# Output projection of a hybrid decoder layer: embedding inputs cast later, x added to h later, the second half's squares summed as rows come, no weight sums ahead of RWKV7's inverses

## The chip, the cores and the metric

The kernel runs on one core of a Trainium2 chip. Five engines work side by side, each in the order of its own queue: TensorE (PE, matrix products, with its weight loads shown apart as PEld), VectorE (DVE), ScalarE (ACT), GpSimd (POOL) and SyncE (SP, which here only issues DMAs). ACT and POOL issue DMAs too; POOL's can add to what stands at their target ("accumulating" ones, the software queue q0). The metric is device time in microseconds, the median of several executions.

## The reference, cut to what matters

One layer, 1024 tokens of width 1024, float32:

```
z = rmsnorm(h) @ w_in                       # 30 column blocks of 128
o_a = hgrn2(z[...]); o_b = dilated_window_attention(z[...]); o_c = rwkv7(z[...])
h = h + concat(o_a, o_b, o_c) @ w_out       # the output projection
h = h + glu_ffn(rmsnorm(h))                 # up, causal conv of width 3, gate, down
h = h + sigmoid(rmsnorm(h) @ ple_gate) * (p @ ple_proj)   # p @ ple_proj: the "embedding"
out = rmsnorm(h)
```

## The kernel before

**Tiles.** Activations are kept transposed, features on 128 partitions and the 1024 tokens along the row; `h` is eight such tiles (h0 to h7), each used as a left and a right half of 512 tokens. Every product is in float32 taken apart into a high part, a cast to a shorter format (`hi`, written by ACT at L124 for weights), and a low part, the rest (`lo`, by DVE or POOL at L130, or at L127 and L128 as an accumulating DMA that subtracts). One product of two 128-blocks is then three matmuls: hi x hi, lo x hi, hi x lo.

**Stages.** `phase_mix` (L339) does the norm, the input projection and the three mixers. `phase_out` (L1323) does the output projection. After it come the FFN and the gated embedding. A tile scheduler sets the order on each engine from the order in which the program is written, from priorities and from dependences. `behind` (L103) adds to instructions an order against a named matmul without a wait on a semaphore: it places them in their queues. `issue_after` keeps PE's own jobs in the written order.

**RWKV7's inverse.** `rwkv_inverse` (L722) runs twice, for the two pairs of heads. It solves small triangular systems on DVE, writes the result to DRAM (Tb to Tz) and reads it back in another layout (Tz to Tc) by SP. The recurrence (`rwkv_main`, small matmuls at L852, the first of them named py and, after one step, pk) begins with Tc. While the inverse runs, `project_rest` (L483) fills PE with the remaining blocks of W_in, six matmuls at a time (a "tick").

**Weight sums.** The output projection is computed with the Strassen-Winograd form of a 2 x 2 block product: seven products p1 to p7 instead of eight, with sums and differences of blocks. The sums of blocks of W_out are made beforehand by `out_sums` (L441): it loads blocks to `wsum` by SP, turns signs on ACT (L450), adds with accumulating DMAs on POOL (L453), and stores the sums to DRAM (the tiles ws1 to ws4). It is a generator that `project_rest` steps at every second tick, after a lead of `LEAD` steps.

**Output projection.** `phase_out` has 28 "jobs", the products p1, p5, p3, p6, p7, p2, p4 with four rows of blocks each. A job (`mul`, L1505, matmuls at L1512) is 12 matmuls of 128 x 512 into one PSUM bank. Banks "a" are two tiles named dp, whose halves serve rows 0 to 3 (rows 0 and 2 share a tile, and rows 1 and 3); banks "b" and "c" are the four tiles zo. Six jobs ahead SP loads the weight (`fetch`, from W_out or from ws); four jobs ahead ACT and DVE take it apart (`weight`). Behind a job the table `extra` places steps by job number:

- `empty` (L1380 to L1385) copies the banks of p1 (ACT, L1384) and p5 (DVE) to h, and at once adds x to each with an accumulating DMA on POOL;
- `load` (L1388) puts x into rows of h that start from it, by SP;
- `gather` (L1390, the addition at L1394 on DVE) adds a bank to h; for p6 and p7 (the left half's last products) it also writes the row out by ACT and sums its squares (`sq_acc`: a square on ACT at L232, an addition on DVE at L233) into `acc`;
- `pair` (L1300 on ACT, L1301 on DVE) takes operands apart;
- `pe_load` (L1487 to L1494) loads a 512 KB block of pT or ple_proj by SP, casts it to `peh` on ACT (L1492), negates that to `pel` (L1493) and adds the block to `pel` by an accumulating DMA (L1494): pT behind jobs 8 and 9, ple_proj behind 18 and 19;
- `factor` and `norm` (jobs 21 and 22) turn the left half's sum of squares into the norm's factor: matmuls with a column of ones (`ps_ss`, L200), a scaling on DVE (L203), a power on POOL (L207), and a spread over the partitions by matmuls (L213). Then DVE scales rows of h by it (L1538) and takes the FFN's operands apart (L1531).

After the jobs the squares of the right half are summed into the same `acc`, row after row, and `embed` (L1469) runs for five blocks of 12 matmuls (L152, L154, L156) in dp tiles; the norm sum of the right half is hooked into it, and three more embedding blocks follow in the banks of the FFN (bv, bg) once the norm's tiles are free.

Of the kernel before, what the change touches and what calls it, by code (L numbers as in the profile page):

```python
# [89 lines left out]
class Trunk:  # L90
# [26 lines left out]

    WB, LEAD = 6, 9

# [321 lines left out]
    def out_sums(self):  # L441
# [14 lines left out]
        for i in range(4):  # L456
            a11, a12, a21, a22 = (wo[m][:, c] for m in (i, 4 + i) for c in (slice(0, HT), slice(HT, T)))
            t, u = (self.spool.tile([P, HT], F32, tag="sqt", name=self.nm("wsum"), bufs=2) for _ in (0, 1))
            nc.sync.dma_start(t, a21)
            nc.sync.dma_start(u, a22)  # L460
            yield from pause(2)
            turn(t)
            add(u, a21)
            yield
            add(t, a11)
            yield from pause(3)
            nc.sync.dma_start(self.S[i]["1"], u)
            nc.sync.dma_start(self.S[i]["3"], t)
            yield
            turn(u)  # L470
            yield
            turn(t)
            add(u, a11)
            yield
            add(t, a22)
            yield
            add(u, a12)
            yield from pause(3)
            nc.sync.dma_start(self.S[i]["2"], t)
            nc.sync.dma_start(self.S[i]["4"], u)  # L480
            yield

    def project_rest(self, js):  # L483
# [4 lines left out]
        for i, j in enumerate(js):  # L488
# [3 lines left out]
            for k in range(ND):  # L492
                self.mm3({0: ps[:, :HT], 1: ps[:, HT:]}, w(k), self.X[k], k == 0, k == ND - 1)
                if k == 3 and i + 1 < len(js):
                    nxt = self.load_w(self.a["w_in"][js[i + 1]])
                if k % 2:
                    with self.behind(self.step):
                        next(self.sums, None)
# [69 lines left out]
    def rwkv(self):  # L568
# [4 lines left out]
        nc.scalar.activation(sg, sg, AF.Sigmoid)  # L573
        self.z = {}
        js = iter((*range(8, 16), 24, 25, 26, 16, 17, 20, 21, 19, 27, 28, 29, 18, 22, 23))
        for p in (0, 1):
# [3 lines left out]
            with tc.tile_pool(name=f"pre{p}", bufs=1) as tp:  # L580
                self.rwkv_prep(p, tp, lt, d, fill)
                self.rwkv_inverse(p, tp, d)
            for i in range(8 * lead - (3 if p else 8)):
                next(fill)
                if p == 0 and i == 1:
                    d["v"] = self.mix_in(4, 4, "v")
                if i == (7 if p else 16):
                    self.rwkv_bonus(d)
            with tc.tile_pool(name=f"rk{p}", bufs=1) as rp:
                self.rwkv_main(p, rp, sg, d, fill)  # L590
            self.rwkv_norm(p, sg, d, 1, fill, 6 - 3 * p)
# [731 lines left out]
    def phase_out(self, hp, x0, emb):  # L1323
# [4 lines left out]
        self.hd = [[self.zpool.tile([P, HT], F32, tag=f"hd{k}_{hf}", name=f"hd{k}_{hf}") for hf in (0, 1)] for k in range(ND)]  # L1328
        acc = hp.tile([P, HT], F32, name="acc")
        wo, V, G = self.a["w_out"], nc.vector, nc.gpsimd  # L1330
        C, D = [[[self.tile16(8 * n + 2 * i + c, F32R) for c in (0, 1)] for i in range(4)] for n in (1, 0)]
        Lo, Eo, A, B = self.Lo, self.Eo, self.A, self.B
# [26 lines left out]
        def sums(m, late):  # L1359
            self.sq_acc(acc, self.h[m][:, right if late else left], m == 0)  # L1360

# [17 lines left out]
        def empty(n, i):  # L1379
            u, x = place(n, i)  # L1380
            if n == "p5":
                V.tensor_copy(u, banks["b"][i])
            else:
                nc.scalar.copy(u, banks["a"][i])  # L1384
            nc.gpsimd.dma_start(u, x, accum_op=ALU.add)  # L1385

# [3 lines left out]
        def gather(n, i):  # L1390
# [4 lines left out]
            if n in ("p6", "p7", "p2", "p4"):  # L1395
                nc.scalar.dma_start(self.hd[m][late], u)
                if n in ("p6", "p7"):
                    sums(m, late)

# [11 lines left out]

        at(4, [lambda i=i: empty("p5", i) for i in range(4)])
        at(5, [lambda i=i: (empty("p1", i), load("p3", i)) for i in range(4)])
        at(16, [lambda i=i: load("p4", i) for i in range(4)])
        at(3, [lambda i=i: self.pair(D[i], Lo[i][1]) for i in range(4)])
# [20 lines left out]
        def factor():  # L1436
            spread.extend(small())
            r.append(self.rstd(spread[0], (acc,)))

        def norm():  # L1440
            self.norm0 = self.ffn_norm(0, self.rstd_spread(r.pop(), spread[1]))

        at(8, [lambda k=k: self.pe_load(px, self.pxp, "pT", k) for k in (0, 1)])
        at(17, [pools, *(lambda k=k: self.pe_load(pw, self.pwp, "ple_proj", k) for k in (0, 1))])
        at(21, [factor, norm])
        at(23, [lambda: [next(self.norm0, None) for _ in (0, 1)] for _ in range(6)])
        tc, self.ends = self.tc, []
        for n, (p, i) in enumerate(jobs):
# [4 lines left out]
            with self.behind(self.ends[-1]):  # L1453
                for go in extra.get(n, ()):
                    go()
        for m in range(ND):
            sums(m, 1)
        ps, pb = small()
        with self.behind(self.ends[23]):
            self.ffn_first()  # L1460
        r = []
        hooks = {(1, 0): lambda: r.append(self.rstd(ps, (acc,))), (1, 1): lambda: self.rstd_spread(r[0], pb)}
        with self.tc.issue_after(self.ends[-1]):
# [20 lines left out]
    def tile16(self, i, dt):  # L1484
        return self.t16.tile([P, HT], dt, tag=f"t{i}", name=self.nm(f"t{i}"), bufs=1)

    def pe_load(self, dst, pool, src, k):  # L1487
        raw = self.ep.tile([P, T], F32, tag="raw", name=self.nm("praw"), bufs=4)
        self.nc.sync.dma_start(raw, self.a[src][k])
        hi, lo = (pool.tile([P, T], F32R, name=self.nm(n)) for n in ("peh", "pel"))  # L1490
# [554 lines left out]
```

## Time and profile before

| What | Value |
| --- | --- |
| Three runs | 1413.71, 1413.72, 1416.59 us; median 1413.72 |
| Profiled execution | 1416.51 us, its span 1414.6 us |
| PE busy | 1372.2 us, 97% of the span, 8598 matmuls |
| DVE, ACT, POOL busy | 1064.8 (75%), 657.6 (46%), 372.0 (26%) |
| Mean granted clock of PE | 0.987 |
| DMA | 192.78 MB; hardware queue q1 155.44 MB, software queue q0 24.65 MB |

The profile's times are those of one execution. Busy time is that of an engine's instructions; PE's matmuls are pipelined, so "busy" at a reduced clock looks like "busy" at full clock, and the clock column tells them apart. An idle time is put down to what ended it, the engine and line whose result came last. In a name such as `h<-h,dp` the output stands ahead of the arrow.

### The profile page before, as it was taken

How to read it: one execution, taken by the hardware profiler on the slowest of the kernel's cores; microseconds unless marked ns; L12 is line 12 of the kernel's file. 1: busy time of each engine (PE TensorE's matmuls, PEld its weight loads, DVE VectorE, ACT ScalarE, POOL GpSimd, SP SyncE). 2: the span in 40 equal slices, each digit the busy share in tenths (PEclk: the TensorE clock that was granted, in tenths of full speed). 3: DMA queues.
4: the chain of work that ended last, by engine and by line, in shares of the span. 5: the costliest groups of instructions: out<-in, count | busy, mean ns of one | idle time of the engine just before them, and what ended most of it. 6: DMA issues, size and time to landing. Idle time of an engine off the chain costs nothing.

```text
span 1414.6 us, 22509 instructions
## 1 busy us (share of the span) xinstructions
PE 1372.2 (97%) x8598; PEld 1113.5 (79%) x8598; DVE 1064.8 (75%) x1664; ACT 657.6 (46%) x1135; POOL 372.0 (26%) x300
## 2 busy tenths in 40 slices
PE   8999999999999999888999999999999999999997
PEld 6878777877878767776888888888888888888886
DVE  7595456825567696678988888898898799777675
ACT  7523433233255584455544344434435444455662
POOL 5211112201221111211245544444553000002231
PEclk9999999999999999989999999999999999999998
DMA  6347533753932211784332232333324963352674
GB/s 229 90 116 172 133 93 88 190 109 107 269 117 98 91 46 46 189 264 171 120 112 99 91 104 103 100 110 112 112 92 138 354 235 101 116 157 65 173 189 153
DMA packets 97114, 192.78 MB, mean 136 GB/s; under 512 B 21872, under 2 KB 24176, under 8 KB 97008
## 3 DMA queue, kind: packets, MB, share of 16 engines
q1 hardware_dynamic: 73408, 155.44, 32.6%
q0 software_dynamic: 12528, 24.65, 9.7%
q10 hardware_dynamic: 11072, 11.28, 2.4%
q8 instruction: 67, 1.10, 0.3%
q14 instruction: 39, 0.32, 0.1%
HBM read 140.73 MB, written 50.59 MB: 135 GB/s over the span
## 4 chain that ended last, share of the span: by engine, by line
PE 53%; issue 3%; DMA 2%; DVE 1%; ACT 1%; POOL 1%; SPq 0%; POOLq 0%; ACTq 0%; DVEq 0%
PE bg L1512 17%; PE bv L1512 13%; PE bv L1814 7%; PE bg L1814 7%; PE bv L152 1%; PE bv L154 1%; PE bv L156 1%; PE bg L152 1%; PE bg L156 1%; PE bg L154 1%; DMA praw<-in_pT_dram 1%; PE zo L1512 1%; DMA wraw<-ws 1%; DMA praw<-in_ple_proj_dram 0%; DVE h L1538 0%
## 5 line engine op out<-in xcount | busy, mean ns | idle before, releaser
L130 POOL TENSOR_TENSOR wlo<-raw,whi 128x512 fp32r<-128x512 f32 x84 | 135.6, 1633 | 75.9 <-ACT whi L124 75.9
L124 ACT CAST whi<-wraw 128x512 fp32r<-128x512 f32 x120 | 73.1, 618 | 153.5 <-PE dp L154 108.9
L152 PE MATMUL dp<-xh,whi 128*128 128x512 f32 x416 | 139.5, 411 | 2.6 <-ACT xh L424 1.8
L156 PE MATMUL dp<-xh,wlo 128*128 128x512 f32 x416 | 132.9, 394 | 0.6 <-POOL wlo L130 0.6
L1512 PE MATMUL bg<-t,whi 128*128 128x512 f32 x352 | 133.4, 389 | 0.0
L154 PE MATMUL dp<-xl,whi 128*128 128x512 f32 x416 | 132.8, 394 | 0.5 <-DVE xl L425 0.5
L130 POOL TENSOR_TENSOR wlo<-s,whi 128x512 fp32r<-128x512 f32 x44 | 64.2, 1460 | 149.7 <-ACT whi L124 149.7
L124 ACT CAST whi<-raw 128x512 fp32r<-128x512 f32 x88 | 52.6, 620 | 91.9 <-issue 48.6
L1814 PE MATMUL bg<-t,whi 128*128 128x512 f32 x308 | 95.1, 390 | 0.0
L1814 PE MATMUL bv<-t,whi 128*128 128x512 f32 x308 | 94.8, 389 | 0.0
L124 ACT CAST whi<-s 128x512 fp32r<-128x512 f32 x66 | 38.9, 620 | 118.9 <-PE bg L1512 113.1
L156 PEld LDWEIGHTS dp<-xh,wlo 128*128 128x128 f32 x416 | 78.4, 189 | 19.7 <-issue 2.0
L154 PEld LDWEIGHTS dp<-xl,whi 128*128 128x128 f32 x416 | 78.8, 189 | 18.9 <-DVE xl L425 1.8
L152 PEld LDWEIGHTS dp<-xh,whi 128*128 128x128 f32 x416 | 75.3, 190 | 22.3 <-issue 5.1
L207 POOL TENSOR_TENSOR rst<-rst,mhalf 128x4 f32<-128x4 f32 (+1 forms) x9 | 9.8, 1089 | 260.6 <-DVE rst L203 244.8
L1512 PEld LDWEIGHTS bg<-t,whi 128*128 128x128 f32 x352 | 66.1, 188 | 13.7
L130 DVE TENSOR_TENSOR wlo<-wraw,whi 128x512 fp32r<-128x512 f32 x74 | 54.4, 739 | 24.8 <-ACT whi L124 16.3
L1810 ACT CAST t<-t 128x512 fp32r<-128x512 f32 x77 | 47.8, 622 | 46.0 <-PE bv L1814 32.8
L1512 PE MATMUL bg<-t,wlo 128*128 128x512 f32 x176 | 67.5, 389 | 0.0
L1814 PEld LDWEIGHTS bv<-t,whi 128*128 128x128 f32 x308 | 57.8, 188 | 11.9
L1814 PEld LDWEIGHTS bg<-t,whi 128*128 128x128 f32 x308 | 57.7, 188 | 11.9
L128 POOL DMA_DIRECT2D wlo<-in_w_in_dram x28 | 24.8, 896 | 140.9 <-ACT wlo L127 138.0
(462 smaller groups left out, 3718.1 us busy)
## 6 DMA issues: line engine op xcount, KB each, us to landing
raw<-in_ffn_up_dram SPq DMA_DIRECT2D x44, 512.0 KB, 3.4
wraw<-in_w_in_dram SPq DMA_DIRECT2D x28, 512.0 KB, 4.0
z<-zst SPq DMA_DIRECT2D x18, 512.0 KB, 3.9
gb<-ct SPq DMA_DIRECT2D x33, 256.0 KB, 2.2
t<-gb SPq DMA_DIRECT2D x33, 256.0 KB, 2.9
t<-gt SPq DMA_DIRECT2D x33, 256.0 KB, 2.6
zl<-z SPq DMA_DIRECT2D x16, 512.0 KB, 4.5
wraw<-in_ple_gate_dram SPq DMA_DIRECT2D x16, 512.0 KB, 3.9
```

The source lines that it names most:

```text
L124: self.cast = nc.scalar.copy(hi, src).ins
L128: nc.gpsimd.dma_start(lo, eng, accum_op=ALU.add)
L130: eng.tensor_tensor(lo, src, hi.bitcast(F32), ALU.subtract)
L152: nc.tensor.matmul(ps[hf], wh, xh[hf], start=first, stop=False)
L154: nc.tensor.matmul(ps[hf], wh, xl[hf], start=False, stop=False)
L156: self.step = nc.tensor.matmul(ps[hf], wl, xh[hf], start=False, stop=last).ins
L207: nc.gpsimd.tensor_tensor(r2, r, self.mhalf[:, :n], ALU.pow)
L1512: self.step = nc.tensor.matmul(ps, w[part == 2][:, s], X[k][part == 1], start=start and k == part == 0, stop=k == 3 and part == 2, skip_gr ...
L1810: nc.scalar.copy(xh, x)
L1814: nc.tensor.matmul(ps[m], wt[part == 2][:, m * P:(m + 1) * P], (xh, xl)[part == 1], start=k == part == 0, stop=k == NK - 1 and part == 2)
```

## The change

**Weight sums.** `LEAD` goes from 9 to 14 and the pauses in `out_sums` grow. `project_rest` steps the sums at every tick unless `self.quiet` is set, which holds for the last 20 ticks ahead of each `rwkv_main`.

**x into h.** All copies of p1 and p5 are ACT's. The accumulating DMAs of x no longer follow each copy: they are placed behind jobs 8 to 11 (p5's rows) and 12 to 15 (p1's rows).

**Squares.** `acc` becomes two accumulators, the second in a tile that is free by then (`xl_5407` in the orders below). Each gather of p2 and p4 (the right half's last products) is followed by its row's square and addition; nothing is left to sum after the jobs.

**Embedding.** Loads (`pe_fetch`) and casts (`pe_load`) are two steps: loads of pT and ple_proj behind jobs 11 to 14, casts behind 16 and 17 (pT) and 19 and 20 (ple_proj). `factor` and `norm` are one job later, 22 and 23.

```
-    WB, LEAD = 6, 9
+    WB, LEAD = 6, 14
...
             nc.sync.dma_start(u, a22)
-            yield from pause(2)
+            yield from pause(3)
             turn(t)
             add(u, a21)
-            yield
+            yield from pause(2)
             add(t, a11)
-            yield from pause(3)
+            yield from pause(5)
             nc.sync.dma_start(self.S[i]["1"], u)
             nc.sync.dma_start(self.S[i]["3"], t)
-            yield
+            yield from pause(2)
             turn(u)
             yield
             turn(t)
             add(u, a11)
-            yield
+            yield from pause(2)
             add(t, a22)
             yield
             add(u, a12)
-            yield from pause(3)
+            yield from pause(5)
...
-                if k % 2:
+                if not self.quiet:
                     with self.behind(self.step):
                         next(self.sums, None)
...
             for i in range(8 * lead - (3 if p else 8)):
+                self.quiet = i >= 8 * lead - 20
                 next(fill)
...
             with tc.tile_pool(name=f"rk{p}", bufs=1) as rp:
+                self.quiet = False
                 self.rwkv_main(p, rp, sg, d, fill)
...
-        acc = hp.tile([P, HT], F32, name="acc")
         wo, V, G = self.a["w_out"], nc.vector, nc.gpsimd
+        acc = [hp.tile([P, HT], F32, name="acc"), self.Lo[0][1]]
...
-            self.sq_acc(acc, self.h[m][:, right if late else left], m == 0)
+            self.sq_acc(acc[late], self.h[m][:, right if late else left], m == 0)
...
         def empty(n, i):
-            u, x = place(n, i)
-            if n == "p5":
-                V.tensor_copy(u, banks["b"][i])
-            else:
-                nc.scalar.copy(u, banks["a"][i])
-            nc.gpsimd.dma_start(u, x, accum_op=ALU.add)
+            nc.scalar.copy(place(n, i)[0], banks[plan[n][1]][i])
+
+        def add_x(n, i):
+            nc.gpsimd.dma_start(*place(n, i), accum_op=ALU.add)
...
-                if n in ("p6", "p7"):
-                    sums(m, late)
+                sums(m, late)
...
+        at(8, [lambda i=i: add_x("p5", i) for i in range(4)])
+        at(12, [lambda i=i: add_x("p1", i) for i in range(4)])
...
-            r.append(self.rstd(spread[0], (acc,)))
+            r.append(self.rstd(spread[0], acc[:1]))
...
-        at(8, [lambda k=k: self.pe_load(px, self.pxp, "pT", k) for k in (0, 1)])
-        at(17, [pools, *(lambda k=k: self.pe_load(pw, self.pwp, "ple_proj", k) for k in (0, 1))])
-        at(21, [factor, norm])
+        pes = [("pT", 0), ("pT", 1), ("ple_proj", 0), ("ple_proj", 1)]
+        at(11, [lambda a=a: self.pe_fetch(*a) for a in pes])
+        at(16, [lambda k=k: self.pe_load(px, self.pxp, "pT", k) for k in (0, 1)])
+        at(18, [pools, *(lambda k=k: self.pe_load(pw, self.pwp, "ple_proj", k) for k in (0, 1))])
+        at(22, [factor, norm])
...
-        for m in range(ND):
-            sums(m, 1)
...
-        hooks = {(1, 0): lambda: r.append(self.rstd(ps, (acc,))), (1, 1): lambda: self.rstd_spread(r[0], pb)}
+        hooks = {(1, 0): lambda: r.append(self.rstd(ps, acc[1:])), (1, 1): lambda: self.rstd_spread(r[0], pb)}
```

What this moves, engine by engine. First POOL's queue from the preparation of the second inverse (`khat`) on: `wlo` are accumulating DMAs of W_in's low parts, `wsum` those of the weight sums. Before:

```order
L685 TENSOR_TENSOR khat_2307<-k_2176,ig_2215 128x1024
L128 DMA wlo_2704<-in_w_in_dram 128x512
L453 DMA wsum_2635<-in_w_out_dram 128x512
L128 DMA wlo_2775<-in_w_in_dram 128x512
L453 DMA wsum_2634<-in_w_out_dram 128x512
L128 DMA wlo_2900<-in_w_in_dram 128x512
L453 DMA wsum_2635<-in_w_out_dram 128x512
L453 DMA wsum_2634<-in_w_out_dram 128x512
L128 DMA wlo_3219<-in_w_in_dram 128x512
L453 DMA wsum_2635<-in_w_out_dram 128x512
L453 DMA wsum_3063<-in_w_out_dram 128x512
```

and in the changed kernel, at the same place:

```order
L687 TENSOR_TENSOR khat_2308<-k_2177,ig_2216 128x1024
L128 DMA wlo_2706<-in_w_in_dram 128x512
L453 DMA wsum_2589<-in_w_out_dram 128x512
L453 DMA wsum_2588<-in_w_out_dram 128x512
L128 DMA wlo_2774<-in_w_in_dram 128x512
L128 DMA wlo_2895<-in_w_in_dram 128x512
L128 DMA wlo_3213<-in_w_in_dram 128x512
L453 DMA wsum_2589<-in_w_out_dram 128x512
L453 DMA wsum_2588<-in_w_out_dram 128x512
L453 DMA wsum_2589<-in_w_out_dram 128x512
L453 DMA wsum_3309<-in_w_out_dram 128x512
```

The sums that stood between the three last `wlo` rows now stand behind the last of them.

Next ACT's queue around jobs 10 to 14 of the output projection, with `whi` a weight's high part, `xh` an operand's, `peh` and `pel` the embedding's input. Before:

```order
L124 CAST whi_6230<-wraw_6162 128x512
L1300 CAST xh_5388<-xh_5404 128x512
L1492 CAST peh_6189<-praw_6187 128x512 x2
L1493 ACTIVATE pel_6190<-peh_6189 128x512 x2
L1300 CAST xh_5390<-xl_5399 128x512
L1492 CAST peh_6220<-praw_6218 128x512 x2
L1493 ACTIVATE pel_6221<-peh_6220 128x512 x2
L124 CAST whi_6251<-wraw_6162 128x512
L1300 CAST xh_5392<-xl_5401 128x512
L124 CAST whi_6273<-wraw_6228 128x512
```

and in the changed kernel:

```order
L124 CAST whi_6204<-wraw_6155 128x512
L1302 CAST xh_5388<-xh_5404 128x512
L124 CAST whi_6226<-wraw_6155 128x512
L1302 CAST xh_5390<-xl_5399 128x512
L124 CAST whi_6251<-wraw_6202 128x512
L1302 CAST xh_5392<-xl_5401 128x512
L124 CAST whi_6277<-wraw_6202 128x512
L1302 CAST xh_5394<-xl_5403 128x512
L1396 DMA hd_0_5927<-h_5919 128x512
```

The embedding's casts are no longer between the operands' casts; they come some 16 rows further on, behind the weights of job 20.

Last DVE at the end of the jobs, up to the gather of h5 from shortly before that of h4 (h_5919 to h_5926 are h0 to h7, dp_5960 and dp_5961 the two dp tiles). Before:

```order
L233 TENSOR_TENSOR acc<-acc,sqt_6701 128x512
L1531 TENSOR_TENSOR t_1102_6428<-h_5920,t_1101_6427 128x512
L1394 TENSOR_TENSOR h_5923<-h_5923,dp_5960 128x512
L1538 SCALAR_TENSOR_TENSOR h_5921<-h_5921,par,ps_ss_6569 128x512
L1538 SCALAR_TENSOR_TENSOR h_5922<-h_5922,par,ps_ss_6569 128x512
L1394 TENSOR_TENSOR h_5924<-h_5924,dp_5961 128x512
```

and in the changed kernel, from the gather of h4 to that of h5:

```order
L1394 TENSOR_TENSOR h_5923<-h_5923,dp_5960 128x512
L233 TENSOR_TENSOR xl_5407<-xl_5407,sqt_6591 128x512
L130 TENSOR_TENSOR wlo_6606<-wraw_6517,whi_6604 128x512
L1542 SCALAR_TENSOR_TENSOR h_5921<-h_5921,par,ps_ss_6595 128x512
L233 TENSOR_TENSOR xl_5407<-xl_5407,sqt_6623 128x512
L1535 TENSOR_TENSOR t_1106_6457<-h_5919,t_1105_6456 128x512
L1535 TENSOR_TENSOR t_1108_6459<-h_5920,t_1107_6458 128x512
L233 TENSOR_TENSOR xl_5407<-xl_5407,sqt_6650 128x512
L1535 TENSOR_TENSOR t_1110_6461<-h_5921,t_1109_6460 128x512
L1542 SCALAR_TENSOR_TENSOR h_5922<-h_5922,par,ps_ss_6595 128x512
L1394 TENSOR_TENSOR h_5924<-h_5924,dp_5961 128x512
```

Two operations stood between the two gathers; now there are nine, three of them additions of squares. (The places on PE: the norm sum stood in the last of the five embedding blocks in dp tiles, and stands in the third of them now, after 26 of the 60 matmuls.)

More of the change, by code (lines that the diff above doesn't have):

```diff
@@ L573, in rwkv @@
         nc.scalar.activation(sg, sg, AF.Sigmoid)
-        self.z = {}
+        self.z, self.quiet = {}, False
         js = iter((*range(8, 16), 24, 25, 26, 16, 17, 20, 21, 19, 27, 28, 29, 18, 22, 23))
@@ L1437, in factor @@
             spread.extend(small())
-            r.append(self.rstd(spread[0], (acc,)))
+            r.append(self.rstd(spread[0], acc[:1]))
         def norm():
             self.norm0 = self.ffn_norm(0, self.rstd_spread(r.pop(), spread[1]))
-        at(8, [lambda k=k: self.pe_load(px, self.pxp, "pT", k) for k in (0, 1)])
-        at(17, [pools, *(lambda k=k: self.pe_load(pw, self.pwp, "ple_proj", k) for k in (0, 1))])
-        at(21, [factor, norm])
+        pes = [("pT", 0), ("pT", 1), ("ple_proj", 0), ("ple_proj", 1)]
[3 more added lines that the diff above has]
+        at(22, [factor, norm])
         at(23, [lambda: [next(self.norm0, None) for _ in (0, 1)] for _ in range(6)])
-        tc, self.ends = self.tc, []
+        tc, self.ends, self.praw = self.tc, [], {}
         for n, (p, i) in enumerate(jobs):
@@ L1485, in tile16, with pe_fetch @@
         return self.t16.tile([P, HT], dt, tag=f"t{i}", name=self.nm(f"t{i}"), bufs=1)
+    def pe_fetch(self, src, k):
+        self.praw[src, k] = raw = self.ep.tile([P, T], F32, tag="raw", name=self.nm("praw"), bufs=4)
+        self.nc.sync.dma_start(raw, self.a[src][k])
     def pe_load(self, dst, pool, src, k):
-        raw = self.ep.tile([P, T], F32, tag="raw", name=self.nm("praw"), bufs=4)
-        self.nc.sync.dma_start(raw, self.a[src][k])
+        raw = self.praw.pop((src, k))
         hi, lo = (pool.tile([P, T], F32R, name=self.nm(n)) for n in ("peh", "pel"))
```

## Prediction

> **What bounds the kernel now.** I read the page first, then the waits of the whole run, then the output phase in windows of 10 us and instruction by instruction, and last the two inverses of RWKV7 side by side. TensorE (PE) is busy for 97% of the span, so time can only be won where PE waits or runs at a reduced clock. Its waits, each with total us, number of times and the longest:
>
> ```profile
> span 1414.6 us, 22509 instructions
> PE dp L1512 <- DVE h L1394: 7.1, 2, 6.6
> PE bv L152 <- DVE h L1538: 4.4, 1, 4.4
> PE py L852 <- DMA Tc<-Tz: 2.9, 2, 1.8
> PE ps_ss L200 <- DVE acc L233: 1.7, 1, 1.7
> ```
>
> The first, second and fourth lie in the output phase, between its first product and the first product of the FFN. The rows below give start, duration, engine, line, operation, and in brackets the idle time before it and its releaser.
>
> ```profile
> 569.27 0.39 PE L1512 MATMUL zo<-xh,whi 128*128 128x512 f32 x1
> 569.43 10.90 PE zo L1512 x48
> 603.26 0.79 PE L1512 MATMUL dp<-xh,whi 128*128 128x512 f32 x1 [6.62 <-DVE h L1394]
> 629.89 1.05 PE L200 MATMUL ps_ss<-few,acc 128*128 128x1 f32 x8 [1.74 <-DVE acc L233]
> 661.32 0.95 PE L200 MATMUL ps_ss<-few,acc 128*128 128x1 f32 x8
> 663.63 0.65 PE L213 MATMUL ps_ss<-cst,rst 128*128 128x128 f32 x4 [0.78 <-POOL rst L207]
> 669.82 1.19 PE L152 MATMUL bv<-peh,peh 128*128 128x512 f32 x2 [4.39 <-DVE h L1538]
> 680.96 1.07 PE L1512 MATMUL bg<-t,whi 128*128 128x512 f32 x4
> ```
>
> The second row (from the chain of waits) prices a matmul without a wait: 10.90 / 48 = 0.227 us. The phase takes 680.96 - 569.27 = 111.7 us. In it stand 24 jobs (the first four were done earlier) and 8 embedding blocks of 12 matmuls, 384 x 0.227 = 87.2, and two norm sums of about 1.2 (0.95 above, and the spread, partly beside other matmuls), 2.4 together: 89.6. So 22.1 us are lost: 7.1 + 1.7 + 0.8 + 4.4 = 14.0 in waits and 8.1 in reduced clock and gaps without a releaser. Windows show that clock (columns: window, its us, busy us and instructions of PE, weight load, DVE, ACT, POOL, then clock, DMA share, GB/s):
>
> ```profile
> 600.00:610.00 10.00, 6.74 (x20) 5.35 (x21) 7.19 (x12) 5.56 (x12) 1.70 (x2) 0.66 0.91 212
> 630.00:640.00 10.00, 10.00 (x43) 8.27 (x44) 4.79 (x9) 4.93 (x10) 2.93 (x4) 0.83 0.99 252
> 650.00:660.00 10.00, 10.00 (x46) 8.29 (x45) 10.00 (x17) 6.17 (x9) 0.00 (x0) 1.00 0.37 146
> 670.00:680.00 10.00, 10.00 (x32) 7.95 (x33) 9.50 (x17) 6.53 (x10) 0.00 (x0) 0.70 0.13 53
> ```
>
> After the 6.62 us wait 20 matmuls took 6.74 (4.5 at 0.227, so 2.2 lost); after the 4.39 wait 32 took 10.0 (7.3, so 2.7 lost). A long wait costs about a third more than its length.
>
> **The change part by part.** (1) *No weight sums ahead of the inverse.* The first inverse of RWKV7 has hardly any sums beside it, the second has; the rows are first use of Tc and the next step.
>
> ```profile
> 134.14 1.20 PE L852 MATMUL py<-Tc,sc 32*32 32x32 f32 x64
> 141.29 0.46 PE L852 MATMUL pk<-KV,AR 64*64 64x64 f32 x16
> 292.34 0.24 PE L852 MATMUL py<-Tc,sc 32*32 32x32 f32 x2 [1.12 <-DMA Tc<-Tz]
> 294.35 1.91 PE L852 MATMUL py<-Tc,sc 32*32 32x32 f32 x62 [1.77 <-DMA Tc<-Tz]
> 304.48 0.46 PE L852 MATMUL pk<-KV,AR 64*64 64x64 f32 x16
> ```
>
> The first stretch takes 141.29 - 134.14 = 7.15, the second 304.48 - (292.34 - 1.12) = 13.26: 6.1 us lost, of which 2.9 are waits for Tc and the rest half clock after them. What differs is the DMA (for each inverse, from Tz written to Tc read: Tc's median us to landing, and packets, MB and share of the accumulating queue):
>
> ```profile
> Tc<-Tz SPq DMA_DIRECT2D x4, 64.0 KB, 2.4
> q0 software_dynamic: 272, 0.51, 19.5%
> Tc<-Tz SPq DMA_DIRECT2D x4, 64.0 KB, 7.5
> q0 software_dynamic: 581, 1.05, 54.3%
> ```
>
> The changed order on POOL puts no accumulating sum between the last weights of the projection and the inverse's end, though W_in's own accumulating rows (wlo) stay there. I keep 0.7 of the 6.1 (0, if Tc lands as in the first inverse, to 3.0, half the loss, if wlo's rows make half of it). The deferred sums come in the recurrence that follows at 304; the output phase that needs them starts at 569, so I cost them at nothing (their harm is a rival).
>
> (2) *Inputs of the embedding later.* The 6.62 wait is one chain:
>
> ```profile
> praw<-in_pT_dram SPq DMA_DIRECT2D x1, 512.0 KB, 13.4
> 594.92 1.14 ACT L1492 CAST peh<-praw 128x512 fp32r<-128x512 f32 x2 [5.37 <-DMA praw<-in_pT_dram]
> 597.65 0.69 DVE L1301 TENSOR_TENSOR xl<-xl,xh 128x512 fp32r<-128x512 f32 x1 [6.10 <-ACT xh L1300]
> 602.52 0.68 DVE L1394 TENSOR_TENSOR h<-h,dp 128x512 f32<-128x512 f32 x1
> ```
>
> ACT works in order. The cast of the embedding's input waits 5.37 us for a load that took 13.4; behind it in ACT's queue stand the casts of B's operands, DVE waits 6.10 for those, and the gather behind them on DVE is late; job 14 writes the dp tile which that gather reads. In the new order these casts stand some 16 rows later on ACT, and their load has long landed: the chain is cut. Next late is a weight slice. SP issues in this order, and the loads land after the given us:
>
> ```profile
> 581.04 0.44 SPq L1388 DMA_DIRECT2D h<-in_xT_dram  x1
> h<-in_xT_dram SPq DMA_DIRECT2D x1, 256.0 KB, 11.2
> 581.52 0.49 SPq L1489 DMA_DIRECT2D praw<-in_pT_dram  x1
> 584.86 0.33 SPq L1343 DMA_DIRECT2D wraw<-ws  x1
> wraw<-ws SPq DMA_DIRECT2D x1, 256.0 KB, 11.9
> ```
>
> The h load landed at 581.04 + 11.2 = 592.2, the 512 KB behind it at 594.9, so they held the queue for 2.7; the weight sum landed at 596.8. Moved ahead of the input it lands at about 594.1. In the new order DVE has its subtraction, two operations and then the gather for job 14 behind it: 594.1 + 0.6 for the cast + 4 operations of about 0.65 is 597.3. Job 14 would start without waits ten jobs after 569.27, at 596.5. I keep 1.0 of this wait (0, since the additions of x also leave jobs 4 to 8 for 8 to 15 and free the queue here, to 3.8, if the sum lands at 596.8 still and DVE has one more operation ahead). p5's four copies of PSUM go from DVE to ACT, which has room (5.56 busy of 10 in the quoted window at 600): nothing, and a small gain if DVE's other work comes sooner.
>
> (3) *Factor and norm a job later.* The 1.74 wait was for squares that DVE had not summed; a job is 12 x 0.227 = 2.72 later, more than 1.74. Gone.
>
> (4) *Squares summed as rows come.* Before, all additions of the second half's squares stand at the end of the jobs or behind them, the last at 659.39, and the scaling of eight rows behind their sum:
>
> ```profile
> 659.39 0.69 DVE L233 TENSOR_TENSOR acc<-acc,sqt 128x512 f32<-128x512 f32 x1
> 664.32 5.36 DVE L1538 SCALAR_TENSOR_TENSOR h<-h,par,ps_ss 128x512 f32<-128x512 f32 x8 [1.85 <-PE ps_ss L213]
> ```
>
> In the new order the norm sum stands on PE after 26 of the embedding's 60 matmuls in this stretch, no longer in the last block: 31 matmuls, 31 x 0.227 = 7.0, follow the spread and cover DVE's 5.36. The 4.39 wait and the 2.7 of reduced clock go. Its price lies on DVE, which was busy for 10.00 of 10.00 at 650 to 660: from the gather of h4 to the last square's addition the new order has 27 DVE operations. At 0.62 us (5.36 / 8 is 0.67, and a subtraction is followed by the next after 0.60) they take 16.7. PE has 62 matmuls between the same points (jobs 25 to 27 and 26 of the embedding), 14.1. DVE is late by 2.6, and by about one operation more since it doesn't start free: 3.4 us of new waits, some 2.0 at job 27, which needs the gather of h5 ten operations after h4's, and 1.4 at the norm sum. Bounds: 0, if DVE runs ahead through the 4.79-of-10 window before, to 7, twice that. The 0.78 wait for POOL's power stays: the row has the same three steps.
>
> New waits are short, yet the 1.74 one was followed by the clock of 0.83 in the row of 630 to 640; I put 1.5 for reduced clock, a third of the 4.4 left at jobs 14 and 27 and the norm sum (0 to 6: both losses of over 2 measured above, with one more). The Trainium skill, page "TensorE: Matmul & The Clock Gate", section "What's actually happening", says that the clock halves after an idle window of about 3.4 us; by that rule the short waits cost no clock, and the sum would be 1391.4. That row speaks against it, so I keep the 1.5.
>
> **Sum.** Lost before: 22.1 + 6.1 = 28.2. Left: 0.7 + 1.0 + 3.4 + 0.8 + 1.5 = 7.4. Gain 20.8. The profiled execution took 1416.51 (span 1414.6 and 1.9 around it), 2.8 above the median of the three runs, 1413.72. It would become 1395.7; on the median, 1413.7 - 20.8 = 1392.9, so 1393. What is late next at the phase's end has slack: DVE splits FFN's sixth operand at 681.0 and PE needs it at 686.4.
>
> ```profile
> 681.02 0.69 DVE L1531 TENSOR_TENSOR tp6l<-nu,tp6h 128x512 fp32r<-128x512 f32 x1
> 686.40 0.39 PE L1512 MATMUL bv<-tp6h,whi 128*128 128x512 f32 x1
> ```
>
> **The rivals.** *DVE keeps up:* only the power's 0.8 is left; gain 27.4, 1386.3. For it: the wait of job 27 rests on a count of operations, and ACT's copies relieve DVE earlier. Against: 10.00 of 10.00. *The middle wait stays:* the DMA share there is 0.91, and the weight or the gather is late for another reason than the cast: 7.1 + 2.2 less the 1.0 kept is 8.3; gain 12.5, 1401.2. *The inverse gains nothing,* because wlo's traffic is enough to slow Tc: gain 20.8 - 5.4 = 15.4, 1398.3. *The change does nothing,* the order being no cause of the waits: 1413.7. *Slower:* the sums, stepped on every tick of six matmuls (1.36 us) instead of every second, turn a sign on ACT three ticks after the load instead of four. The loads of those tiles (wsum) landed after, at least, in the median and at most:
>
> ```profile
> DMA to landing us min/median/max: 2.0/4.3/9.1
> ```
>
> Three ticks are 4.1 us; a load that lands after 9.1 holds ACT's queue for 5.0, behind it W_in's casts, and PE waits with 2.0 of slow clock after it. Four such turns cost 28.0, more than 20.8: 1413.7 + 7.2 = 1420.9. It decides if ACT's wait reaches PE on three of the four turns; against it speaks the median of 4.3, and the weights cast a block ahead.
>
> **How the numbers follow.** Forecast 0.56, DVE keeps up 0.13, middle wait stays 0.14, inverse gains nothing 0.09, nothing happens 0.03, slower 0.05. A difference of 0.2% is 2.8 us, about the least that a measurement here tells from none; the first four cases lie beyond it: faster 0.92, same 0.03, slower 0.05. The range goes from 1386, everything gone, to 1403: the middle wait or the inverse's loss may stay with some of the residuals at their upper ends; it leaves out the last two cases and the sums of several bad ends.
>
> **What would show it.** Right: no wait of PE over 2 us between 569 and the FFN; Tc landing in under 4 us in the second inverse; the norm sum at about two fifths of the embedding; the phase near 96 us (89.6 and the 6.7 left of it). Wrong: a wait of 5 us or more at job 14 still (step 2), a wait at job 27 above 4 (step 4), or 304.48's step still 13 after the first use of Tc (step 1); or new waits for weights between 300 and 560.

## The result, and the profile after

| | us |
| --- | --- |
| Before, 4 runs | median 1414.22 (1413.71 to 1416.59) |
| Changed, 4 runs | median 1405.07 (1402.42 to 1406.92) |
| Ratio | 0.9931, 95% interval 0.9908 to 0.9953 |
| Changed, a second series of 6 | median 1402.66 beside 1412.18 before; ratio 0.9935, interval 0.9922 to 0.9948 |

The change saves 9.2 us, 0.7%. The forecast was 20.8. The sign is right, the size is less than half, and the time of the first series lies outside the range (the median of the second, 1402.66, just inside it).

The profiled execution of the changed kernel took 1406.92 (span 1405.0), 1.9 above its median; before it was 1416.51, so the two traces differ by 9.6, close to the medians' difference, and can be taken apart. PE's longest waits in it from 560 to 700 us (total, times, longest):

```profile
PE dp L152 <- DVE h L1394: 3.6, 1, 3.6
PE bv L1516 <- POOL wlo L130: 2.2, 1, 2.2
PE dp L1516 <- DVE h L1394: 2.1, 1, 2.1
PE bv L1516 <- ACT whi L124: 1.9, 1, 1.9
PE ps_ss L213 <- POOL rst L207: 0.9, 1, 0.9
PE bg L1516 <- ACT e L1609: 0.7, 1, 0.7
```

None of the four waits of before that were to go is left: no 6.62 at job 14, no 1.74 at the first norm sum, no 4.39 behind the second, no wait for Tc. Three of those listed are in the output phase (2.1 at job 27, 3.6 at the first embedding block, 0.9 for POOL's power, which was 0.8 before), three lie behind it, at the FFN's start. The FFN goes through its weights in units; the last row below is the first product that unit 1 has to itself. Some of PE's instructions, in order of time, from job 4 to there:

```profile
564.12 0.39 PE L1516 MATMUL zo<-xh,whi 128*128 128x512 f32 x1
630.35 0.47 PE L1516 MATMUL dp<-xh,whi 128*128 128x512 f32 x1 [2.09 <-DVE h L1394]
636.98 1.22 PE L152 MATMUL dp<-peh,peh 128*128 128x512 f32 x2 [3.62 <-DVE h L1394]
648.51 0.65 PE L213 MATMUL ps_ss<-cst,rst 128*128 128x128 f32 x4 [0.92 <-POOL rst L207]
664.24 1.07 PE L1516 MATMUL bg<-t,whi 128*128 128x512 f32 x4
678.98 0.50 PE L1516 MATMUL bv<-tp6h,wlo 128*128 128x512 f32 x1 [2.20 <-POOL wlo L130]
686.18 0.47 PE L1516 MATMUL bv<-tp7h,whi 128*128 128x512 f32 x1 [1.92 <-ACT whi L124]
698.76 0.39 PE L1516 MATMUL bg<-tp5h,whi 128*128 128x512 f32 x1
```

The last of these is this one in the kernel before:

```profile
708.41 0.39 PE L1512 MATMUL bg<-tp5h,whi 128*128 128x512 f32 x1
```

So the difference can be followed along the program. Job 4 starts at 564.12 instead of 569.27: 5.2 won upstream. The output phase takes 664.24 - 564.12 = 100.1 instead of 111.7: 11.6 won. The stretch from there to unit 1 takes 698.76 - 664.24 = 34.5 instead of 708.41 - 680.96 = 27.5: 7.1 lost again. Together 9.7; the spans differ by 9.6. In the second profile of the same kernel (`changed_again` below) the phase takes 98.1 and the stretch 32.9.

The second inverse in the changed kernel (first use of Tc, the next step, Tc's landing, the accumulating queue meanwhile):

```profile
289.67 1.20 PE L854 MATMUL py<-Tc,sc 32*32 32x32 f32 x64
297.70 0.46 PE L854 MATMUL pk<-KV,AR 64*64 64x64 f32 x16
```

```profile
q0 software_dynamic: 281, 0.51, 20.9%
Tc<-Tz SPq DMA_DIRECT2D x4, 64.0 KB, 3.6
```

The step takes 8.0 where it took 13.3, with the queue at 20.9% instead of 54.3% and Tc landing after 3.6 instead of 7.5. That alone is 5.2, but it isn't the whole of what stands between the two profiles at job 4: the changed one is 1.6 ahead when the step begins (1.0 of it already at the first inverse), and it loses 1.6 again between the step and job 4. In its window from 505 to 515 us the granted clock is 0.83; it is 1.00 in the second profile and before, and the second profile loses nothing between the step and job 4.

### The profile page after: what moved, and what is told of

It is laid out like the page before. It is cut to its first block, busy times and chain, and to the rows that moved or that the text cites. A ratio compares the mean times of both kernels' runs of the same rounds, so it can differ in the third digit from the quotient of the medians.

```text
span 1405.0 us, 22501 instructions
## 1 busy us (share of the span) xinstructions
PE 1368.0 (97%) x8598; PEld 1110.4 (79%) x8598; DVE 1065.4 (76%) x1660; ACT 660.1 (47%) x1139; POOL 370.9 (26%) x300
## 4 chain that ended last, share of the span: by engine, by line
PE 80%; issue 8%; DVE 7%; POOL 2%; ACT 2%; DMA 0%; SPq 0%; POOLq 0%; DVEq 0%; ACTq 0%
PE bg L1516 16%; PE bv L1516 13%; PE bv L1818 7%; PE bg L1818 7%; PE dp L152 6%; PE dp L154 6%; PE dp L156 6%; PE bv L152 1%; PE bv L156 1%; PE bv L154 1%; PE bg L152 1%; PE bg L156 1%; PE bg L154 1%; DVE ig L648 1%; PE zp L152 1%
```

## The experiments

Two theories were held against each other. *Theory A*: the time was given back through the order of the work around the norm, by an ACT cast that waits for a load and by weights of the FFN that are now prepared late. *Theory B*: DVE has too much to do from job 24 to unit 1, in whatever order. "Stretch" is the time from the FFN's first product to unit 1's own, as above.

Two readings of the trace led to A. The first is ACT and DVE around 630 us, ahead of the 3.62 wait:

```profile
630.96 0.62 ACT L124 CAST whi<-raw 128x512 fp32r<-128x512 f32 x1 [3.84 <-DMA raw<-in_ffn_up_dram]
632.52 0.62 ACT L1534 CAST t<-h 128x512 fp32r<-128x512 f32 x1
```

```profile
633.17 0.69 DVE L1535 TENSOR_TENSOR t<-h,t 128x512 fp32r<-128x512 f32 x1 [2.31 <-ACT t L1534]
636.25 0.68 DVE L1394 TENSOR_TENSOR h<-h,dp 128x512 f32<-128x512 f32 x1
```

It is the chain that the change removed at job 14, in a new place: ACT waits for a load of a weight that PE uses only at 664, an operand's cast stands behind it, DVE waits for that operand, and the gather stands behind DVE's wait. The second reading is where the FFN's weight sums (s, raw) stand. In the changed kernel, on DVE and then on POOL:

```profile
649.20 5.36 DVE L1542 SCALAR_TENSOR_TENSOR h<-h,par,ps_ss 128x512 f32<-128x512 f32 x8 [1.03 <-PE ps_ss L213]
670.49 0.69 DVE L1629 TENSOR_TENSOR s<-s,raw 128x512 f32<-128x512 f32 x1
```

```profile
675.24 3.69 POOL L130 TENSOR_TENSOR wlo<-s,whi 128x512 fp32r<-128x512 f32 x1 [26.78 <-ACT whi L124]
```

and in the kernel before:

```profile
657.52 0.69 DVE L1625 TENSOR_TENSOR s<-s,raw 128x512 f32<-128x512 f32 x1
```

```profile
663.56 1.27 POOL L130 TENSOR_TENSOR wlo<-s,whi 128x512 fp32r<-128x512 f32 x1
```

Before, DVE made the sum 6.8 us ahead of the norm's scaling (664.32), between the late squares, and POOL had split it before PE came out of its 4.39 wait. Now it comes 21 us behind the start of the scaling, and the FFN waits for it. The split itself is slow there too, 3.69 instead of 1.27: it ends at 678.93 and PE goes on at 678.98, while PE's matmul before it began at 676.39. With the old 1.27 it would have ended at 676.5, so the wait of 2.2 is made of both, the late start and the slow split beside DVE's subtractions (the last section has more on that).

**The weights ahead of the norm** (`weights_ahead`). The edit, in `ffn_first`; the unit's own code then uses what is there:

```
         for d in self.units[:2]:
             d["w1"] = self.split2(d["raw"][:, :HT], self.nc.vector)
+        with self.behind(self.ends[27]):
+            for d in self.units[:2]:
+                d["w2"] = self.split2(d["raw"][:, HT:], self.nc.vector)
+            d = self.units[0]
+            self.up_sums(d)
+            d["pre"] = {n: self.split2(d["s"][n], self.nc.gpsimd) for n in "65"}
...
```

> The changed kernel, with the splits and sums of the FFN's first weights (second halves of units 0 and 1, the three sums of unit 0 and the splits of two of them) put behind the last job, ahead of the norm's scaling, where they stood before the change. Theory A (time is given back at the FFN's start, because these sums now stand on DVE behind the norm's work, so that POOL's and ACT's splits come late): the waits of 2.2 and 1.9 us at the FFN's start go, the stretch from the FFN's first matmul to unit 1's first product falls from 34.5 to about 28, and the time from 1405.1 to 1398 to 1401. Rival B (DVE has too much work there, whatever its order): the waits only change their place, the stretch stays above 33, the time within 1.5 of 1405.1.

Measured: 1399.37, ratio 0.9903 (0.9886 to 0.9920). Its waits of PE:

```profile
PE dp L152 <- DVE h L1394: 3.1, 1, 3.1
PE dp L1516 <- DVE h L1394: 2.1, 1, 2.1
PE bv L1516 <- DVE bv L1697: 1.3, 1, 1.3
```

Both waits for the weights are gone, the stretch is 29.0 (from 659.75 to 688.71 on PE), the waits of the output phase stand. A is right on the FFN's start. (POOL's split of the same sum takes 1.28 in its new place, so the edit removes both its lateness and its slowness.)

**The casts behind the last job** (`cast_behind_last_job`):

```
-        for d in self.units[:2]:
-            d["w1"] = self.split2(d["raw"][:, :HT], self.nc.vector)
+        with self.behind(self.ends[27]):
+            for d in self.units[:2]:
+                d["w1"] = self.split2(d["raw"][:, :HT], self.nc.vector)
```

> The changed kernel, with the casts of the FFN's first two weights placed on ACT behind job 27 instead of job 23, nothing else. Theory A (ACT, in order, waits 3.8 us there for a load and holds up the operand casts that DVE needs ahead of the gather of h6): the wait of 3.62 at the first embedding block falls to 1.3 or less, the stretch from job 4 to the FFN from 100.1 to 96 to 98; the time falls by 1 to 4, to 1401 to 1404, unless the FFN's start gives it back. Rival B (DVE has too much work): the 3.6 stays within 1.

Measured: 1398.73, ratio 0.9898 (0.9882 to 0.9915), more than A expected. PE's waits of over 1 us in it, from job 4 on:

```profile
PE bv L1516 <- POOL wlo L130: 2.2, 1, 2.2
PE dp L1516 <- ACT t L1534: 2.1, 1, 2.1
```

The wait at the embedding has gone as a whole and the phase takes 95.0; the FFN's start still pays (stretch 33.0). A is right here too.

**Both together** (`both_reorders`, the two edits above).

> Both edits together: first weights' casts behind job 27, and the second halves' splits and unit 0's sums ahead of the norm. Theory A: both losses go, 1395 to 1399. Rival B: 1403 to 1406.

Measured: 1398.68, ratio 0.9901 (0.9884 to 0.9917): no better than either alone, at A's upper end of 1399 and far from B's 1403. The phase takes 94.0, yet the stretch 32.3. What PE waits for is now this:

```profile
PE bv L1516 <- DVE bv L1698: 3.0, 1, 3.0
PE dp L1516 <- ACT t L1534: 2.1, 1, 2.1
PE dp L152 <- DVE h L1394: 1.3, 1, 1.3
```

L1698 is unit 0's last addition on DVE, behind the whole chain of scalings and operands. By this reading the next limit is DVE itself, and B gets its due for the remainder; whether that is DVE's amount of work or again its order, two later runs ask.

**Weight sums alone** (`sums_quiet_alone`): the kernel before with `LEAD`, the pauses, the stepping and `quiet` as changed, nothing of the output phase.

> The kernel before, with only the weight sums' new timing (lead, pauses, every tick, none in the last 20 ticks ahead of the recurrence). Forecast's first step: the stretch from the second inverse's first use of Tc to the next step falls from 13.3 to 7 to 8, the time by 5.4, 1408.3 to 1410. Rival (W_in's own accumulating rows slow Tc as much): stretch still 12 or more, the time within 1 of 1414.2. Rival (sums on every tick hold up ACT elsewhere): a gain under 3 with new waits of PE between 300 and 560.

Measured: 1410.22, ratio 0.9974 (0.9963 to 0.9986), 3.7 us won (2.0 to 5.2), less than the 5.4 expected. The step behind the second inverse:

```profile
289.75 1.20 PE L854 MATMUL py<-Tc,sc 32*32 32x32 f32 x64
297.76 0.46 PE L854 MATMUL pk<-KV,AR 64*64 64x64 f32 x16
```

8.0, as in the changed kernel, and the output phase as slow as before (111.2). Of the waits that the rival foretold for 300 to 560 us only one of 0.4 came. But this profile too has the clock of 0.83 from 505 to 515 us and loses 1.7 between the step and job 4; whether that explains the rest of the 5.4 in all twelve runs isn't shown.

**Squares at the end again** (`squares_at_end`), all else as changed:

```
                 nc.scalar.dma_start(self.hd[m][late], u)
-                sums(m, late)
+                if n in ("p6", "p7"):
+                    sums(m, late)
...
+        for m in range(ND):
+            sums(m, 1)
         ps, pb = small()
```

> The changed kernel without its squares part: the second half's squares are summed after the jobs again (into the second accumulator), all else as changed. Theory A (the earlier norm sum gains 7 in the output phase, but costs 2.1 and 3.6 of waits with slow clock behind them, and 7.1 at the FFN's start): without it the waits at job 27 and at the first embedding block go, the 4.4 one at the fourth-last product of the phase is back, the FFN's stretch is 27.5 again, and from job 4 to unit 1 it takes about 127 where the changed kernel takes 134.6: 1397 to 1400, faster than the changed kernel. By the forecast's sum this part is worth 3 to 4: 1408 to 1409.

Measured: 1400.48, ratio 0.9900 (0.9884 to 0.9915), against 0.9931 and 0.9935 of the changed kernel. So the squares' part, as it was made, cost 4 to 5 us (1 to 8 by the intervals), where the forecast's sum had it win 3.7: the 4.39 wait and 2.7 of clock, less the 3.4 of new waits. (`x_adds_early`, the next kernel, which takes as long as the changed one, was measured beside this one and is 5.9 above it.) Its waits:

```profile
PE bv L152 <- DVE h L1545: 5.5, 1, 5.5
PE dp L1519 <- DVE h L1394: 2.5, 1, 2.5
PE ps_ss L213 <- POOL rst L207: 1.4, 1, 1.4
```

The wait that the part was to remove is back, 5.5 here, and yet the time is less: the stretch is 27.5 again, and the wait at the first embedding block is gone. A had not expected the 2.5: ACT's cast of a late slice of W_out waited 4.2 for its load there. From job 4 to unit 1 it takes 131.6 here, where A had put 127; it is 134.6 in the changed kernel's first profile and 131.0 in its second, so single profiles don't show the cost, and the verdict rests on the series.

**x added early** (`x_adds_early`): the additions of x follow their copies at once, at jobs 4 to 8.

```
             nc.scalar.copy(place(n, i)[0], banks[plan[n][1]][i])
+            add_x(n, i)
...
-        at(8, [lambda i=i: add_x("p5", i) for i in range(4)])
-        at(12, [lambda i=i: add_x("p1", i) for i in range(4)])
```

> The changed kernel, but each addition of x follows its copy at once, at jobs 4 to 8, as before the change. Theory (ACT's cast in front of the operands made the 6.6 us wait, so casting later alone removes it): no wait over 1 us at job 14, time within 1.5 of 1405.1. Rival (the full DMA queue made it, and moving the additions away is what helped): a wait of 2 to 7 us at jobs 12 to 16, 1408 to 1414.

Measured: 1406.33, ratio 0.9942 (0.9929 to 0.9954): not to be told from the changed kernel. The 6.62 wait stays away (0.57 is left of it). Moving the additions did no measurable part of it; what is left is the chain on ACT that the trace before shows. (p5's copies are ACT's here too. That they left DVE was not tried apart.)

**Squares on POOL** (`squares_on_gpsimd`): both reorders, and

```
-    def sq_acc(self, acc, src, first):
+    def sq_acc(self, acc, src, first, eng=None):
...
-            nc.vector.tensor_tensor(acc, acc, t, ALU.add)
+            (eng or nc.vector).tensor_tensor(acc, acc, t, ALU.add)
...
-            self.sq_acc(acc[late], self.h[m][:, right if late else left], m == 0)
+            self.sq_acc(acc[late], self.h[m][:, right if late else left], m == 0, G if late else None)
```

> Both reorders of the earlier run, and the second half's additions of squares moved from DVE to POOL. Theory B, as it stands after those runs (DVE's amount of work from job 24 to unit 1 is the next limit): DVE loses seven operations of 0.6, 4.2 us; the waits at job 27 (2.1) and the first embedding block (1.3) go, the 3.0 one at unit 0's last product shrinks, 1394 to 1397 against 1398.7. Rival (POOL and DVE slow each other: a sum on DVE beside POOL's split took 1.66 instead of 0.69): no gain, 1398 to 1400, with DVE's additions above 1 us beside POOL's.

Measured: 1396.22, ratio 0.9874 (0.9861 to 0.9888). The waits at job 27, at the first embedding block and at unit 0's addition are gone; the additions on POOL take 1.30 to 1.95 each, and the rival's slowing shows too (below), without eating the gain.

**Gathers first** (`gathers_first`): both reorders, and

```
-            V.tensor_tensor(u, u, banks[g][i], ALU.add)
+            with self.tc.high_priority(offset=400 if n == "p4" else 0):
+                V.tensor_tensor(u, u, banks[g][i], ALU.add)
```

> Both reorders of the earlier run, and the gathers of the last product ahead of DVE's other ready work. If the order of DVE's operations is what costs 2.1 at job 27 and 1.3 at the first embedding block: both go, and the time falls by 3 or more, 1395 to 1396. If DVE's amount of work is the limit: those waits go, the norm sum or the FFN's start waits longer instead, and the time stays within 1.5 of 1398.7.

Measured: 1395.54, ratio 0.9868 (0.9854 to 0.9881), the best of the kernels tried and under both of the originals. DVE has the same work, so most of what was left was order as well, and not its amount. PE's waits of over 1 us from job 4 on:

```profile
PE bv L152 <- DVE h L1543: 2.8, 1, 2.8
PE bv L1517 <- DVE bv L1699: 1.4, 1, 1.4
PE ps_ss L213 <- POOL rst L207: 1.3, 1, 1.3
```

The gathers' waits have gone, and DVE's scalings of the norm are the longest that is left.

**All three** (`gathers_first_gpsimd`): that and the squares on POOL.

> All three arrangements together: both reorders, the last product's gathers first on DVE, the second half's additions of squares on POOL. If DVE's order and its amount of work each cost on their own: 1392 to 1394, under both 1395.5 (gathers first) and 1396.2 (squares on POOL). If they are two ways to the same time (gathers no longer behind squares): 1395 to 1397.

Measured: 1397.30, ratio 0.9886 (0.9868 to 0.9904): no addition, and 0.3 above the upper case's range. They are two ways to the same time, as far as these intervals tell.

**The end rearranged** (`end_rearranged`): squares at the end, the casts behind job 27, gathers first.

> The squares at the end (as before the change) with the other parts of the change, the casts of the FFN's first weights behind job 27 and the last product's gathers first on DVE: what the squares' part is worth when the rest is arranged for either. Theory A (the earlier norm sum is a gain of some us that was lost to the order of the work around it): 1398 to 1401, 3 to 5 above the 1395.5 of the same arrangement with squares as rows come. Rival (the squares' part is worth nothing even when well arranged): 1394 to 1397.

Measured: 1399.05, ratio 0.9896 (0.9882 to 0.9911), above 0.9868 (0.9854 to 0.9881) of the same gathers with squares as rows come. The earlier norm sum is worth some 4 us by these ratios once the work around it is arranged (2.8 in the two profiles, from job 4 to unit 1); the intervals only just part. This kernel lacks the early weights of `gathers_first`, but doesn't need them, since its stretch is 28.3 without and 29.5 there.

**Gathers first only** (`gathers_first_only`): the changed kernel with that one edit.

> The changed kernel with one edit: the gathers of the last product ahead of DVE's other ready work. Theory A: the waits of 2.1 at job 27 and 3.6 at the first embedding block go without touching ACT, since the gathers no longer stand behind the operations that wait for ACT; the output phase takes 94 to 96. The FFN's first weights are still split behind the norm's work, the stretch to unit 1 stays 31 to 35. Time 1398 to 1402. Rival (ACT's wait for the load holds the phase up in any order): the 3.6 stays, 1404 to 1406.

Measured: 1399.33, ratio 0.9907 (0.9893 to 0.9922). The phase takes 92.3, the least of all and under the 94 to 96 expected, and the stretch 35.2, the most of all:

```profile
PE bg L1517 <- ACT e L1610: 2.8, 1, 2.8
PE bv L1517 <- DVE bv L1690: 2.6, 1, 2.6
PE bv L152 <- DVE h L1543: 2.1, 1, 2.1
```

What the phase wins is given back in part at the FFN, as in the changed kernel itself.

**The changed kernel again** (`changed_again`), for its interval:

> The changed kernel once more, beside the run above on the same chip: 1403 to 1406.5, ratio 0.992 to 0.995, if the earlier rounds stand.

Measured: 1402.66, ratio 0.9935, the second series in the table above. Its profile has the same waits, with 2.8 instead of 3.6 at the first embedding block and 0.3 instead of 1.9 for `whi` at the FFN.

## Why the prediction was wrong, point by point

- *Inverse (1): right in its mechanism, too large in its size.* Tc's late landing was the sums' doing, as a kernel with only that edit shows, and the step lost its 5.2. The whole part won 3.7 (2.0 to 5.2) in its series, against 5.4. That job 4 also starts 5.2 earlier in the first profile is chance: 1.6 won ahead of the step and 1.6 lost behind it cancel.
- *Embedding's inputs (2) and factor (3): right.* 1.0 was kept of the wait at job 14; 0 was left. With the inverse, these parts give 0.9900, 14.1 us; less the 3.7 that is 10.4, against 10.0 forecast (7.1 + 2.2 - 1.0 for the inputs and 1.7 for the factor). Each of the two measured terms is known to 2 us only, so the closeness is in part luck. The reason given held: with the additions of x back on the queue the wait stayed away.
- *New waits on DVE in the phase (4): the place right, the size not.* Job 27 was put at 2.0 and took 2.1. The next was put at 1.4 at the norm sum; it came at the first embedding block and was 3.6, because of a cast on ACT that the count of DVE's operations didn't contain: it stands ahead of an operand's cast and waits 3.84 for `ffn_first`'s load, where the kernel before waited for no such load. (The count itself was right, 27 operations.) Reduced clock and gaps came to 3.9 (100.1 less 89.6 and the waits of 6.6), not 1.5; 2.9 of it is one place, the 14 matmuls behind the 3.62 wait, which took 6.1. Together 3.8 more than the 6.7 kept for the phase. The forecast's "about a third more" for a long wait was a misreading of its own figures: 2.2 on 6.62 is a third, 2.7 on 4.39 is three fifths, and 2.9 on 3.62 here is four fifths.
- *"What is late next at the phase's end has slack": this step failed.* It looked at one operand, tp6, and at its 5.4 us. The FFN needs weights too. Before, DVE summed them between the late squares, and POOL split them while the norm's factor was made and PE waited; in the changed kernel's order two of unit 0's three sums and both splits stand behind the norm's scaling. 7.1 us came back there (5.4 in the second profile, 32.9 less 27.5), with waits of 2.2, 1.9 and 0.7 and reduced clock. That putting the weights ahead takes the stretch from 34.5 to 29.0 shows it.
- *The net.* By the two profiles the forecast missed by 11.2 (20.8 against 9.6): 7.1 at the FFN's start, which it had put at nothing, 3.8 in the phase, 0.2 upstream. By the series it missed by 11.6: the squares' part was to win 3.7 and cost 4 to 5 instead, some 8 together, and the inverse gave 1.7 less; what is left, some 2, is about the clock that the sum counted as won outside these places (8.1 less 2.2, 2.7 and the 1.5 kept).
- *The signs.* Of the signs of being right, Tc's landing (3.6) and the early norm sum came; no wait over 2 us and a phase near 96 did not. None of the signs of being wrong came: all of them lie ahead of the FFN, where the largest loss was.
- *The rivals.* None had this mechanism. The nearest in time was "the middle wait stays", with 1401.2, and its cause was wrong. The slower case (sign turns of the weight sums that hold up ACT) came half true: in the changed kernel ACT waits twice at a turn, at 116 and 120 us, where it didn't before, but for a store of the sums and not for their load,

```profile
ACT wsum L450 <- DMA ws<-wsum: 5.5, 2, 4.0
```

  and the first recurrence behind them still begins 1.0 earlier than before (133.10 instead of 134.14). PE has no wait between 300 and 560 us that it had not before by more than 0.4.

The stretch is 34.5 in the first profile of the changed kernel and 32.9 in the second because reduced clock falls in another place. The wait for `whi` ends 7.2 behind the wait for `wlo` in both (678.98 to 686.18, and 675.30 to 682.49), so ACT and DVE set that time. In the second profile PE's matmuls right behind the `wlo` wait are 0.43 apart until 679.05, which uses up all but 0.3 of the `whi` wait. In the first they are 0.23 apart there, PE waits 1.9, and the slow matmuls come behind that wait, where nothing hides them.

What stays open: why the scheduler moved the sums; and how much of the 2.8 that PE still waits for DVE's scalings in `gathers_first` could go.

## What to carry to other kernels

When a change removes a wait, list what other engines did during it and just ahead of it: work that was free there (here weight sums and their splits) has to go somewhere, and it can become the next thing waited for. On an engine that works in order, a cast that waits for a load is the load's wait for all that stands behind it; so tie such casts to the place of their use. Then put what releases another engine's buffers (the gathers) ahead of work that has time.

## What the runs showed of the hardware

**The clock after short waits.** In the changed kernel the 2.09 wait at 630.35 was followed by 12 matmuls in 2.9 us, full clock up to the next wait, and the 1.92 wait at 686.18 was followed by matmuls of 0.23 for 1.2 us and then of 0.43 for 3.4 us:

```profile
687.18 0.44 PE L1516 MATMUL bv<-tp7l,whi 128*128 128x512 f32 x1
687.42 0.63 PE L1516 MATMUL bv<-tp7h,wlo 128*128 128x512 f32 x1
687.85 0.63 PE L1516 MATMUL bv<-tp7h,whi 128*128 128x512 f32 x1
...
690.41 0.58 PE L1516 MATMUL bg<-tp3h,whi 128*128 128x512 f32 x1
690.83 0.39 PE L1516 MATMUL bg<-tp3l,whi 128*128 128x512 f32 x1
```

So a wait of 1.92 us can cost clock, and one as long may not. Two profiles of this same kernel show it at one place: waits of 1.11 at 508.2 and 0.56 at 509.5 stand in both, and the granted clock from 505 to 515 us is 0.83 in the first and 1.00 in the second. The length of the slow stretch, 687.4 to 690.8, is the 3.4 us that the Trainium skill (page "TensorE: Matmul & The Clock Gate", section "What's actually happening") gives for its free-running window; its condition of an idle window of that length is not what these rows show.

**DVE and POOL.** With the squares on POOL, DVE's additions and subtractions of two SBUF tiles stopped while POOL had one in hand:

```profile
637.39 1.66 DVE L1570 TENSOR_TENSOR s<-s,raw 128x512 f32<-128x512 f32 x1
638.97 0.68 DVE L130 TENSOR_TENSOR wlo<-raw,whi 128x512 fp32r<-128x512 f32 x1
640.17 1.78 DVE L130 TENSOR_TENSOR wlo<-raw,whi 128x512 fp32r<-128x512 f32 x1
```

```profile
636.55 1.94 POOL L233 TENSOR_TENSOR xl<-xl,sqt 128x512 f32<-128x512 f32 x1 [2.85 <-ACT sqt L232]
639.78 1.63 POOL L130 TENSOR_TENSOR wlo<-s,whi 128x512 fp32r<-128x512 f32 x1 [1.28 <-ACT whi L124]
```

POOL's end at 638.49 and DVE's at 639.05, POOL's at 641.41 and DVE's at 641.95: each time DVE ended 0.55 behind POOL, about the length of its own operation. It goes the other way too: in the changed kernel POOL's split at 675.24 took 3.69 beside four subtractions of DVE (675.31 to 677.81, 2.50); 1.27, its length elsewhere, and 2.50 make 3.77. The Trainium skill, page "SBUF — State Buffer", section "Terms", says that the two engines share a port pair and that the loser blocks for the whole instruction; these rows agree.
